# Modulation sections as one accumulating run of eight matmuls, in a diffusion backbone on one core

## The chip, the cores and the metric

The kernel runs on one NeuronCore of a Trainium2 chip. The metric is the device time of one execution in microseconds. Before the change it is 837.59 us, the median of three runs between 837.31 and 838.25.

## The reference

Two layers work on 512 latent tokens and 256 context tokens of width 1024. Each layer normalizes its input, scales and shifts it, mixes tokens, and adds a gated, normalized result:

```python
shift, scale, gate = adaln(c, ada_w[i], ada_b[i])        # silu(c) @ w + b, split in three
cshift, cscale, cgate = adaln(c_ctx, ada_w[i], ada_b[i])
h = rms_norm(x, pre_g[i]) * (1.0 + scale) + shift
y, yc = mixer_i(h, hc, ...)                               # 0: differential attention, 1: grouped-query attention
x = x + gate * rms_norm(y, post_g[i])
```

The change concerns `adaln`, the modulation: two vectors of 1024 (`c` and `c_ctx`) times a matrix of 1024 x 3072 per layer, in float32.

## The kernel before

**Tiling.** Activations lie with features on the 128 partitions, in eight blocks (`KT`). A weight block is loaded as float32 (`raw`, two buffers), split by a cast on ScalarE (`whi`, line 206) and a subtraction on GpSimd or VectorE (`wlo`, line 200), and used in three matmuls per block (lines 146 to 148, `mm3`). All weight loads are issued on SP's queue in a fixed order (`WStream`); three pairs of split buffers hold them, and a pair is refilled when its last matmul has released it.

**Stages.** First come the normalization and the modulation of layer 0's shift and scale (`ada_pe`, `cols4`, line 462). Then, up to about 470 us, layer 0's attention, where the change is. Then the output projection of layer 0, the whole of layer 1, and its output projection.

**Layer 0's attention.** Eight heads, one after the other. A unit is 128 queries against all keys: 12 score matmuls into a pair of double banks (line 868), two row maxima on VectorE (873), two exponentials on ScalarE (876), reciprocals, a scaling on GpSimd (214) and a combination on VectorE (884) that gives the probabilities `p`. Both double banks are used by each unit, so the next unit's scores need both exponentials done. Two units' probabilities are transposed on TensorE (line 933), evicted as a split pair `ah` (ScalarE, 936) and `al` (VectorE, 937), and multiplied with the values (line 153). At the end of a head a column sum of squares (lines 374 and 375, with ScalarE and GpSimd making its split pair in lines 372 and 373) normalizes the head's output. In between, as filler, TensorE projects the queries, keys, values and gates of later heads.

**What sets the order.** A planner (`flow`) keeps a clock of planned TensorE time and calls steps when they are due; each step has a cost, lags behind other steps and a time `at`. Fillers run when nothing is due. Single banks are handed out in rotation, the least recently used first (`trp` and `pj`, four banks). What the planner emits is then put into each engine's queue by a list scheduler that uses priorities and its own timeline. Each engine runs its queue in order.

**The modulation's later sections.** The six remaining sections of 512 columns (gates of layer 0, shift and scale of layer 1) are computed during heads 2 to 7. A section is two groups (`g`) of four matmuls, each group over 512 input features; `grp_load` loads 1 MB per group into `araw` (one buffer), on SP's queue. In `grp_mm` the four matmuls of a group go to the four column quarters of the array: matmul `j` multiplies the 32-column stationary `s32[:, 4*g+j]` with 512 columns and writes partitions 32j to 32j+31 of one bank. `after(prev)` keeps the four in order; other TensorE work may be placed between them. The first group's bank is copied to `arow` by ScalarE (line 727), the second group's bank is added to it by VectorE (line 730). Then the group's buffer is loaded again. `ada1_finish` (line 737) and `gate0_finish` (line 1002) sum the four quarters with one more matmul each and put the result into its place. `ACCN` says how many of these steps go to which head: three in each of heads 2 to 7 (two `grp_mm`, one finish), spaced evenly over the head.

Of the kernel before, what the change touches and what calls it, by code (L numbers as in the profile page):

```python
# [9 lines left out]
F32 = mybir.dt.float32  # L10
F32R = mybir.dt.float32r
AF = mybir.ActivationFunctionType
ALU = mybir.AluOpType
# [3 lines left out]
P = 128  # L17
# [12 lines left out]
HF0 = ((('qk', 1), ('qk', 2), ('z', 0)), (('qk', 3),), (('z', 1), ('v', 2), ('qk', 4), ('z', 2)), (('qk', 5), ('z', 3)), (('v', 4), ('qk', 6), ('z', 4)), (('qk', 7), ('z', 5)), (('v', 6), ('z', 6)), (('z', 7),))  # L30
FILL0 = tuple(f for hf in HF0 for f in hf)
ATT = 15.0
ACCN = (0, 0, 3, 3, 3, 3, 3, 3)
ACD = 5.0
FILL1 = (('z', 0), ('q', 2), ('q', 1), ('z', 2), ('z', 1), ('q', 3), ('z', 3), ('z', 4), ('z', 5), ('z', 7), ('z', 6))
HOT0 = (4200, 3100, 0, 4800)
# [48 lines left out]
def tile_backbone(  # L85
# [20 lines left out]
    nc = tc.nc  # L106
    uid = [0]

    def nm(s):
        uid[0] += 1  # L110
        return f"{s}_{uid[0]}"
# [178 lines left out]
    def after(prev):  # L290
        return nullcontext() if prev is None else tc.issue_after(prev.ins)
# [123 lines left out]
    def mod_cols(layer, half, which, psrc):  # L415
        for v in range(2):
            src = psrc(v)
            dst = mods[:, layer, v, which, half * 4:half * 4 + 4]
            b = abT[:, layer, which, half * 4:half * 4 + 4]
            if which == 0:  # L420
                nc.vector.tensor_tensor(dst, src, b, ALU.add)
            else:
                nc.vector.scalar_tensor_tensor(dst, src, 1.0, b, ALU.add, ALU.add)
                nc.vector.tensor_tensor(dst, dst, pre[:, layer, half * 4:half * 4 + 4], ALU.mult)
# [24 lines left out]
    s32 = cp.tile([P, KT, 32], F32, name="s32", bufs=1)  # L449
# [254 lines left out]

    with tc.tile_pool(name="t0", bufs=1) as t0:
        SECS = ((0, 4), (0, 5), (1, 0), (1, 2), (1, 1), (1, 3))
        groups = [(layer, sec, g) for layer, sec in SECS for g in range(2)]
        loaded, rows = {}, {}

        def grp_load(i):  # L710
            if i < len(groups):
                layer, sec, g = groups[i]
                t = loaded[i] = t0.tile([P, 4, 512], F32, tag="araw", name=nm("araw"), bufs=1)
                nc.sync.dma_start(
                    t, ada_w[layer, g * 512:(g + 1) * 512, sec * 512:(sec + 1) * 512].rearrange("(k p) n -> p k n", p=P))

        def grp_mm(i):
            layer, sec, g = groups[i]
            t = loaded.pop(i)
            o = trp()  # L720
            prev = None
            for j in range(4):
                with after(prev):
                    prev = nc.tensor.matmul(o[32 * j:32 * j + 32, :], s32[:, 4 * g + j, :], t[:, j, :], start=True, stop=True)
            if g == 0:
                r = rows[layer, sec] = t0.tile([P, 512], F32, tag="arow", name=nm("arow"), bufs=1)
                nc.scalar.copy(r, o)
            else:
                r = rows[layer, sec]
                nc.vector.tensor_tensor(r, o, r, ALU.add)  # L730
            grp_load(i + 1)

        def ada1_finish(layer, sec):
            r = rows.pop((layer, sec))
            o = trp()
            for b in range(4):
                nc.tensor.matmul(o[:, 2 * b:2 * b + 2], r[:, b * P:(b + 1) * P], sel32, start=b == 0, stop=b == 3)
            ov_ = o[:, :8].rearrange("p (k v) -> p v k", v=2)
            mod_cols(layer, sec % 2, sec // 2, lambda v: ov_[:, v, :])
# [30 lines left out]
        def qr_tile():  # L770
            return t0.tile([P, T], F32, tag="qr", name=nm("qr"), bufs=4)
# [223 lines left out]
        def gate0_finish(half):  # L995
            r = rows.pop((0, 4 + half))
            sl = slice(half * 512, half * 512 + 512)
            b = bcast(ada_b[0, 2 * D + half * 512:2 * D + half * 512 + 512])
            g = bcast(post_g[0, sl])
            for v in range(2):  # L1000
                o = trp()
                nc.tensor.matmul(o, selb[v], r, start=True, stop=True)
                nc.vector.tensor_tensor(gate0[v][:, sl], o, b, ALU.add)
                nc.vector.tensor_tensor(gate0[v][:, sl], gate0[v][:, sl], g, ALU.mult)
# [15 lines left out]
        for which, o in enumerate((oq, ok)):  # L1020
            r = qr_tile()
# [11 lines left out]
            add({"qk": qk_proj, "v": v_proj, "z": z_proj}[kind](i))  # L1033
        def acc_steps():
            res = []
            grp_load(0)
            for i, (layer, sec, g) in enumerate(groups):
                res.append(Step(lambda i=i: grp_mm(i), 1.5, hot=False))
                if g:
                    f = (lambda sec=sec: gate0_finish(sec - 4)) if layer == 0 else (lambda layer=layer, sec=sec: ada1_finish(layer, sec))  # L1040
                    res.append(Step(f, 2.0 if layer == 0 else 1.0, [(res[-1], ACD)], hot=False))
            return res

        A_ = acc_steps()
        S_, T_, M_, X_ = [], [], [], []
        at_ = clock[0] + FZ
# [38 lines left out]
        for h in range(KT):  # L1085
            per = ATT + DL0[h] + sum(7.7 if f[0] == 'z' else 15.4 for f in HF0[h] if f != ('qk', 1))
            span = per - GAP0
            lo, hi = sum(ACCN[:h]), sum(ACCN[:h + 1])
            for i in range(lo, min(hi, len(A_))):
# [35 lines left out]
            at_ += per  # L1125
        for st_ in A_[sum(ACCN):]:
            st_.at = at_
# [35 lines left out]
    for qi, (c, n) in enumerate(OUTC[:2]):  # L1163
# [4 lines left out]
        for m in order:  # L1168
            v = 0 if m < NQ else 1
            o = pj(n) if qi else o_pre[m]  # L1170
# [12 lines left out]
    c, n = OUTC[2]  # L1183
# [47 lines left out]
    for i, m in enumerate(order):  # L1231
        o = pj(n)
# [11 lines left out]
    with tc.tile_pool(name="t1", bufs=1, side="right") as t1p:  # L1244
# [61 lines left out]
        for what, m in KV:  # L1306
# [146 lines left out]
        def gate1_part(half, k2):  # L1453
            acc = gate1[:, half * 512:half * 512 + 512]
            gw = wp.tile([P, 1024], F32, tag="raw", name=nm("raw"), bufs=2)
            nc.sync.dma_start(
                gw.rearrange("p (k n) -> p k n", k=2),
                ada_w[1, k2 * 256:(k2 + 1) * 256, 2 * D + half * 512:2 * D + half * 512 + 512].rearrange("(k p) n -> p k n", p=P),
            )
            for k in range(2):  # L1460
                kt = k2 * 2 + k
                gs = gw[:, k * 512:(k + 1) * 512]
                if kt == 0:
                    VP[EGA].tensor_scalar(acc, gs, scol[:, 0, kt:kt + 1], None, ALU.mult)
                else:
                    VP[EGA].scalar_tensor_tensor(acc, gs, scol[:, 0, kt:kt + 1], acc, ALU.mult, ALU.add)

        def gate1_finish(half):
            acc = gate1[:, half * 512:half * 512 + 512]
            o = pj(512)  # L1470
            colsum(o, acc, [t1q.tile([P, 512], F32R, tag=t, name=nm("ac"), bufs=n) for t, n in (("za", 1), ("sz", 2))])
            b = wp.tile([P, 1024], F32, tag="raw", name=nm("raw"), bufs=2)
            sl = slice(half * 512, half * 512 + 512)
            nc.sync.dma_start(b[:, :512], ada_b[1, 2 * D + half * 512:2 * D + half * 512 + 512].partition_broadcast(P))
            nc.sync.dma_start(b[:, 512:], post_g[1, sl].partition_broadcast(P))
            nc.vector.tensor_tensor(acc, o, b[:, :512], ALU.add)
            close(o)
            nc.vector.tensor_tensor(acc, acc, b[:, 512:], ALU.mult)
# [33 lines left out]
        for h in range(KT):  # L1512
            p, j = h // 2, h % 2
# [17 lines left out]
        for i in range(10):  # L1531
            f = (lambda i=i: gate1_part(i // 5, i % 5)) if i % 5 < 4 else (lambda i=i: gate1_finish(i // 5))
# [10 lines left out]
        for qi, (c, n) in enumerate(OUTC1):  # L1543
# [4 lines left out]
            for m in range(NQ):  # L1548
                o = pj(n) if qi else o_pre[m]
# [12 lines left out]
                if qi == 2:  # L1562
                    r = rstd_sum(ss[m][:, 2:3], ss[m][:, 0:1])
# [95 lines left out]
```

## Time and profile before

| | |
|---|---|
| median of three runs | 837.59 us |
| the profiled execution, its own time | 836.02 us |
| its span, first to last instruction | 834.0 us |
| mean granted TensorE clock | 0.992 |
| TensorE busy | 797.1 us, 96% of the span |
| VectorE, ScalarE, GpSimd busy | 58%, 55%, 52% |
| line 724, the sections' matmuls | 48 matmuls, 96 records, from 163.7 to 421 us |
| line 730, VectorE's additions | 6 of about 0.69 us |
| line 714, the sections' loads | 12 of 1 MB, 5.5 us from issue to landing |

The span is shorter than the execution's own time by 2.0 us, which lie around it. In the profile a float32 matmul stands as two records, one for each pass, and each record's length is a modelled time from start to end; matmuls overlap, so distances between starts tell what one costs. "Busy" adds up stretches in which at least one instruction runs. In the rows of the timeline the first number is the start in us, the second the length in us; "x8" is the number of records merged in a row. In rows that group instructions by line, three numbers with slashes are the shortest, median and longest duration in ns. In the waits, the numbers are the total in us, how often, and the longest in us.

### The profile page before, as it was taken

How to read it: one execution, taken by the hardware profiler on the slowest of the kernel's cores; microseconds unless marked ns; L12 is line 12 of the kernel's file. 1: busy time of each engine (PE TensorE's matmuls, PEld its weight loads, DVE VectorE, ACT ScalarE, POOL GpSimd, SP SyncE). 2: the span in 40 equal slices, each digit the busy share in tenths (PEclk: the TensorE clock that was granted, in tenths of full speed). 3: DMA queues.
4: the chain of work that ended last, by engine and by line, in shares of the span. 5: the costliest groups of instructions: out<-in, count | busy, mean ns of one | idle time of the engine just before them, and what ended most of it. 6: DMA issues, size and time to landing. Idle time of an engine off the chain costs nothing. (4 is left out here: it accounts for less than half of the span.)

```text
span 834.0 us, 14405 instructions
## 1 busy us (share of the span) xinstructions
PE 797.1 (96%) x5482; PEld 705.2 (85%) x5482; DVE 484.2 (58%) x897; ACT 458.7 (55%) x1001; POOL 437.0 (52%) x538
## 2 busy tenths in 40 slices
PE   7999999999999999999999999989998989999997
PEld 5788887798878898778988898779998779889986
DVE  4434576764857425665377843674266677665634
ACT  5424357674574644764467643754364656666731
POOL 4444755865475743765633212585776836723201
PEclk9899999999999999999999999999999999999999
DMA  9934211222133321414310051031232240300112
GB/s 302 353 112 140 76 39 47 63 95 70 71 102 127 114 76 64 151 42 153 124 51 26 27 202 51 26 108 51 77 99 79 81 153 21 102 26 26 64 38 101
DMA packets 41540, 77.77 MB, mean 93 GB/s; under 512 B 3584, under 2 KB 18688, under 8 KB 41472
## 3 DMA queue, kind: packets, MB, share of 16 engines
q1 hardware_dynamic: 38048, 71.71, 26.0%
q10 hardware_dynamic: 3424, 5.15, 1.8%
q8 instruction: 43, 0.70, 0.3%
q14 instruction: 25, 0.20, 0.1%
HBM read 70.56 MB, written 2.10 MB: 87 GB/s over the span
## 5 line engine op out<-in xcount | busy, mean ns | idle before, releaser
L200 POOL TENSOR_TENSOR wlo<-raw,whi 128x256 fp32r<-128x256 f32 x200 | 150.6, 784 | 89.1 <-ACT whi L206 75.6
L146 PE MATMUL bk<-whi,h 128*128 128x256 f32 (+1 forms) x592 | 177.0, 302 | 6.2 <-DVE u L1191 1.8
L147 PE MATMUL bk<-wlo,h 128*128 128x256 f32 (+1 forms) x592 | 176.3, 299 | 0.2 <-DVE wlo L200 0.2
L148 PE MATMUL bk<-whi,h 128*128 128x256 f32 (+1 forms) x592 | 175.0, 298 | 0.9 <-DVE h L1229 0.8
L146 PE MATMUL bk<-h,whi 128*128 128x512 f32 (+2 forms) x416 | 147.7, 355 | 2.4 <-ACT sq L965 1.5
L148 PE MATMUL bk<-h,wlo 128*128 128x512 f32 (+2 forms) x416 | 144.9, 349 | 0.1
L147 PE MATMUL bk<-h,whi 128*128 128x512 f32 (+2 forms) x416 | 144.9, 349 | 0.0
L146 PEld LDWEIGHTS bk<-whi,h 128*128 128x128 f32 x592 | 112.6, 190 | 16.4 <-issue 4.2
L147 PEld LDWEIGHTS bk<-wlo,h 128*128 128x128 f32 x592 | 112.6, 190 | 4.3 <-issue 0.5
L148 PEld LDWEIGHTS bk<-whi,h 128*128 128x128 f32 x592 | 111.9, 190 | 5.1 <-DVE h L1229 1.5
L214 POOL TENSOR_SCALAR p<-p,sm 128x768 f32<-128x768 f32 (+1 forms) x80 | 68.2, 855 | 82.0 <-DVE sm L879 34.6
L146 PEld LDWEIGHTS bk<-h,whi 128*128 128x128 f32 x416 | 78.2, 188 | 15.3 <-issue 4.5
L206 ACT CAST whi<-raw 128x1024 fp32r<-128x1024 f32 x64 | 67.4, 1053 | 37.2 <-DMA raw<-in_b_w 15.1
L148 PEld LDWEIGHTS bk<-h,wlo 128*128 128x128 f32 x416 | 78.1, 188 | 8.7 <-issue 1.3
L147 PEld LDWEIGHTS bk<-h,whi 128*128 128x128 f32 x416 | 78.3, 188 | 7.0 <-issue 0.8
L876 ACT ACTIVATE p<-sc,sm 128x768 f32<-128x768 f32 (+1 forms) x68 | 59.7, 882 | 29.4 <-DVE sm L873 28.7
L873 DVE TENSOR_REDUCE sm<-sc 128x1 f32<-128x768 f32 (+1 forms) x68 | 60.5, 919 | 22.2 <-PE sc L868 22.2
L184 POOL TENSOR_TENSOR sz<-sz,za 128x384 f32<-128x384 f32 (+1 forms) x24 | 28.1, 1173 | 39.3 <-ACT za L183 39.3
L936 ACT CAST ah<-bk 128x512 fp32r<-128x512 f32 x56 | 31.8, 592 | 29.5 <-PE bk L933 23.6
L937 DVE TENSOR_TENSOR al<-bk,ah 128x512 fp32r<-128x512 f32 x56 | 37.6, 684 | 16.0 <-ACT ah L936 15.5
L868 PE MATMUL sc<-qk,qk 64*128 64x384 f32 (+1 forms) x396 | 46.1, 355 | 0.2 <-POOL qk L768 0.2
L1430 DVE TENSOR_TENSOR al<-bk,ah 128x512 fp32r<-128x512 f32 x48 | 32.3, 685 | 23.0 <-ACT ah L1429 23.0
(245 smaller groups left out, 1700.1 us busy)
## 6 DMA issues: line engine op xcount, KB each, us to landing
raw<-in_a_w SPq DMA_DIRECT2D x30, 512.0 KB, 3.6
araw<-in_ada_w SPq DMA_DIRECT2D x12, 1024.0 KB, 5.5
raw<-in_b_w SPq DMA_DIRECT2D x20, 512.0 KB, 3.5
ag<-in_ada_w SPq DMA_DIRECT2D x32, 256.0 KB, 6.7
raw<-in_w_out SPq DMA_DIRECT2D x16, 512.0 KB, 3.5
sw<-qr ACTq DMA_DIRECT2D x32, 128.0 KB, 2.1
raw<-in_ada_w SPq DMA_DIRECT2D x8, 512.0 KB, 3.6
xt<-in_x SPq DMA_DIRECT2D x4, 512.0 KB, 5.3
```

Of the source, the lines that this page charges most:

```text
L146: nc.tensor.matmul(o, ahi, bhi, start=start, stop=False)
L147: nc.tensor.matmul(o, ahi, blo, start=False, stop=False)
L148: nc.tensor.matmul(o, alo, bhi, start=False, stop=stop)
L200: eng.tensor_tensor(dst[:, i:i + n], a[:, i:i + n], b[:, i:i + n], op)
L206: nc.scalar.copy(hi, r)
L214: (nc.vector if eng == "v" else nc.gpsimd).tensor_scalar(dst, src, s_, 1.0, ALU.mult, ALU.mult)
L868: prev = nc.tensor.matmul(sc[m][:, j if nk == T else m, :w], a[r, tok], b[r, c], start=i == 0, stop=i == 2)
L873: nc.vector.tensor_reduce(mx, scv, AX.XY if nk == T else AX.X, ALU.max, negate=True)
L876: nc.scalar.activation(pv_, scv, AF.Exp, bias=mx, accum_out=l[:, m:m + 1])
L936: nc.scalar.copy(ah, tr)
L937: nc.vector.tensor_tensor(al, tr, f32(ah), ALU.subtract)
L1430: nc.vector.tensor_tensor(al, tr, f32(ah), ALU.subtract)
```

## The change

One step now computes a whole section: eight matmuls, two to each column quarter, of which the second accumulates onto the first in the same bank (`start` only for `g == 0`, `stop` only for `g == 1`). The section's two loads are issued one after the other into two `araw` buffers. One copy by ScalarE evicts the bank; the addition by VectorE is gone. The step costs 2.2 in the planner's clock where the two steps cost 1.5 each, and `ACCN` gives two steps per head instead of three.

```diff
-ACCN = (0, 0, 3, 3, 3, 3, 3, 3)
+ACCN = (0, 0, 2, 2, 2, 2, 2, 2)
...
-        def grp_load(i):
-            if i < len(groups):
-                layer, sec, g = groups[i]
-                t = loaded[i] = t0.tile([P, 4, 512], F32, tag="araw", name=nm("araw"), bufs=1)
-                nc.sync.dma_start(
-                    t, ada_w[layer, g * 512:(g + 1) * 512, sec * 512:(sec + 1) * 512].rearrange("(k p) n -> p k n", p=P))
-
-        def grp_mm(i):
-            layer, sec, g = groups[i]
-            t = loaded.pop(i)
+        def sec_load(i):
+            if i < len(SECS):
+                layer, sec = SECS[i]
+                loaded[i] = [t0.tile([P, 4, 512], F32, tag="araw", name=nm("araw"), bufs=2) for _ in range(2)]
+                for g, t in enumerate(loaded[i]):
+                    nc.sync.dma_start(
+                        t, ada_w[layer, g * 512:(g + 1) * 512, sec * 512:(sec + 1) * 512].rearrange("(k p) n -> p k n", p=P))
+
+        def sec_mm(i):
             o = trp()
             prev = None
-            for j in range(4):
-                with after(prev):
-                    prev = nc.tensor.matmul(o[32 * j:32 * j + 32, :], s32[:, 4 * g + j, :], t[:, j, :], start=True, stop=True)
-            if g == 0:
-                r = rows[layer, sec] = t0.tile([P, 512], F32, tag="arow", name=nm("arow"), bufs=1)
-                nc.scalar.copy(r, o)
-            else:
-                r = rows[layer, sec]
-                nc.vector.tensor_tensor(r, o, r, ALU.add)
-            grp_load(i + 1)
+            for g, t in enumerate(loaded.pop(i)):
+                for j in range(4):
+                    with after(prev):
+                        prev = nc.tensor.matmul(
+                            o[32 * j:32 * j + 32, :], s32[:, 4 * g + j, :], t[:, j, :], start=g == 0, stop=g == 1)
+            r = rows[SECS[i]] = t0.tile([P, 512], F32, tag="arow", name=nm("arow"), bufs=1)
+            nc.scalar.copy(r, o)
+            sec_load(i + 1)
...
-            for i, (layer, sec, g) in enumerate(groups):
-                res.append(Step(lambda i=i: grp_mm(i), 1.5, hot=False))
-                if g:
...
+            for i, (layer, sec) in enumerate(SECS):
+                res.append(Step(lambda i=i: sec_mm(i), 2.2, hot=False))
...
```

The finishing step follows each section's step as before.

More of the change, by code (lines that the diff above doesn't have):

```diff
@@ L706, in tile_backbone @@
         SECS = ((0, 4), (0, 5), (1, 0), (1, 2), (1, 1), (1, 3))
-        groups = [(layer, sec, g) for layer, sec in SECS for g in range(2)]
         loaded, rows = {}, {}
-        def grp_load(i):
-            if i < len(groups):
-                layer, sec, g = groups[i]
-                t = loaded[i] = t0.tile([P, 4, 512], F32, tag="araw", name=nm("araw"), bufs=1)
-                nc.sync.dma_start(
-                    t, ada_w[layer, g * 512:(g + 1) * 512, sec * 512:(sec + 1) * 512].rearrange("(k p) n -> p k n", p=P))
-        def grp_mm(i):
-            layer, sec, g = groups[i]
-            t = loaded.pop(i)
+        def sec_load(i):
[6 more added lines that the diff above has]
+        def sec_mm(i):
             o = trp()
             prev = None
-            for j in range(4):
-                with after(prev):
-                    prev = nc.tensor.matmul(o[32 * j:32 * j + 32, :], s32[:, 4 * g + j, :], t[:, j, :], start=True, stop=True)
-            if g == 0:
-                r = rows[layer, sec] = t0.tile([P, 512], F32, tag="arow", name=nm("arow"), bufs=1)
-                nc.scalar.copy(r, o)
-            else:
-                r = rows[layer, sec]
-                nc.vector.tensor_tensor(r, o, r, ALU.add)
-            grp_load(i + 1)
+            for g, t in enumerate(loaded.pop(i)):
[6 more added lines that the diff above has]
+            sec_load(i + 1)
         def ada1_finish(layer, sec):
@@ L1035, in acc_steps @@
             res = []
-            grp_load(0)
-            for i, (layer, sec, g) in enumerate(groups):
-                res.append(Step(lambda i=i: grp_mm(i), 1.5, hot=False))
-                if g:
-                    f = (lambda sec=sec: gate0_finish(sec - 4)) if layer == 0 else (lambda layer=layer, sec=sec: ada1_finish(layer, sec))
-                    res.append(Step(f, 2.0 if layer == 0 else 1.0, [(res[-1], ACD)], hot=False))
+            sec_load(0)
+            for i, (layer, sec) in enumerate(SECS):
+                res.append(Step(lambda i=i: sec_mm(i), 2.2, hot=False))
+                f = (lambda sec=sec: gate0_finish(sec - 4)) if layer == 0 else (lambda layer=layer, sec=sec: ada1_finish(layer, sec))
+                res.append(Step(f, 2.0 if layer == 0 else 1.0, [(res[-1], ACD)], hot=False))
             return res
```

## The prediction

> **What bounds the kernel now.** I read the page's busy shares first, then the busy times of the stretch that holds the change, then TensorE's waits in it.
>
> ```profile
> PE 797.1 (96%) x5482; PEld 705.2 (85%) x5482; DVE 484.2 (58%) x897; ACT 458.7 (55%) x1001; POOL 437.0 (52%) x538
> PEclk9899999999999999999999999999999999999999
> ```
>
> ```profile
> 110.00:430.00 320.00, 316.07 (x2228) 272.08 (x2227) 190.41 (x332) 187.12 (x393) 193.82 (x193) 1.00 0.27 88
> 430.00:470.00 40.00, 36.55 (x269) 33.88 (x267) 35.25 (x60) 30.26 (x64) 11.41 (x11) 1.00 0.08 27
> ```
>
> ```profile
> PE bk L933 <- DVE al L937: 1.9, 2, 1.6
> PE bk L375 <- POOL sqs L373: 1.6, 1, 1.6
> PE bk L146 <- ACT sq L965: 1.5, 1, 1.5
> PE bk L724 <- DVE al L937: 0.9, 1, 0.9
> PE bk L724 <- DVE gT L214: 0.6, 1, 0.6
> ...
> PE sc L868 <- POOL qk L768: 0.2, 1, 0.2
> ```
>
> The windows give length, then busy time of TensorE, its weight loads, VectorE, ScalarE and GpSimd. TensorE is the bound, and the clock granted to it is full (1.00 in both windows): in layer 0's attention it is idle for 320 - 316.07 = 3.9 us of 320, and in the last head (430 to 470 us) for 3.4 of 40. The waits (total, times, longest, from 67 to 470 us) explain most of it. No other engine passes 61% up to 430 us; in the last head VectorE reaches 35.25 of 40, so an eviction there waits its turn. So two things move the time: how long TensorE's own instructions take, and new or removed waits, which can save at most these 7.4 us.
>
> **The matmuls of the modulation.** They are 48 before and after, each a float32 matmul of 512 columns on one quarter of the array, recorded as two passes. Layer 0's first sections do the changed form already (L462): eight matmuls (x8 records are four matmuls, x16 eight) accumulating in one bank.
>
> ```profile
> 27.07 0.28 PE L148 MATMUL bk<-whi,h 128*128 128x256 f32 x1
> 27.28 1.06 PE L462 MATMUL bk<-ag,s 128*32 128x512 f32 x8
> 28.27 0.39 PE L146 MATMUL bk<-whi,h 128*128 128x256 f32 x1
> 28.61 0.28 PE L148 MATMUL bk<-whi,h 128*128 128x256 f32 x1
> ...
> 37.05 0.28 PE L147 MATMUL bk<-wlo,h 128*128 128x256 f32 x1
> 37.17 0.28 PE L148 MATMUL bk<-whi,h 128*128 128x256 f32 x1
> 37.37 1.92 PE L462 MATMUL bk<-ag,s 128*32 128x512 f32 x16
> 39.23 0.51 PE L146 MATMUL sc<-h,whi 128*128 128x256 f32 x2
> 39.57 0.28 PE L146 MATMUL bk<-whi,h 128*128 128x256 f32 x1
> ```
>
> ```profile
> 247.56 1.06 PE L724 MATMUL bk<-araw,s 128*32 128x512 f32 x6
> 248.55 0.66 PE L933 MATMUL bk<-ident,p 128*128 128x128 f32 x4
> 249.13 1.04 PE L724 MATMUL bk<-araw,s 128*32 128x512 f32 x2
> 250.11 0.50 PE L146 MATMUL bk<-h,whi 128*128 128x512 f32 x1
> ```
>
> Projection matmuls of 256 columns follow each other every 0.12 us (37.05, 37.17). From the L148 at 27.07 to the one at 28.61 are three such steps, 0.36 us; 1.54 passed, so a group of four costs 1.18. From 37.17 to 39.57 are again three steps; 2.40 passed, so a run of eight costs 2.04. The second four in a run thus cost 0.86, and getting in and out of the form 0.32. Whole runs would cost 6 x 2.04 = 12.2 us, against 12 x 1.18 = 14.2 for twelve whole groups.
>
> But neither program keeps them whole. The split group at 247.56 shows the price: its lone fourth matmul holds TensorE from 249.13 to 250.11, 0.98 us, as long as four (27.28 to 28.27). What counts is rounds of up to four quarters. The changed program's order on TensorE splits four of the six runs: 3+5, 6+2, 8, 4+4, 6+2, 8 matmuls, with scores, transposes or column sums between the parts. That is 10 entries and 3+3+2+2+3+2 = 15 rounds, against 13 entries and 13 rounds now (eleven groups of four, one of 3+1). Before: 13 x 1.18 = 15.3; after: 10 x 1.18 + 5 x 0.86 = 16.1. **+0.8 us**: the run costs more than the groups it replaces.
>
> Counting the changes of form alone, the sum would be 3 x 0.32 = 1.0 us less. The Trainium skill (TensorEngine Tiling (Array Packing), Key Properties) says that changing the tiling mode drains TensorE, and that tiles work independently; the 0.32 us agrees with the drain, and the lone matmul's 0.98 says that an unfilled round eats what the fewer drains save.
>
> **Banks, the copy and the add.** Each section takes one bank where it took two.
>
> ```profile
> L727 ACT COPY arow<-bk x6: 576/587/609, 166.4 to 411.9; 128x512 f32<-128x512 f32 x6
> L730 DVE TENSOR_TENSOR arow<-bk,arow x6: 676/688/692, 193.7 to 422.7; 128x512 f32<-128x512 f32 x6
> ```
>
> The six adds go: 6 x 0.69 = 4.1 us of VectorE, beside TensorE and worth nothing by themselves; the six copies stay. The two waits of L724 for a bank (0.9 and 0.6 above) should go: in the changed order at least 3 us of TensorE work lie between a bank's former use and a section's first matmul. Ends 0 and -1.5; I take **-1.5**.
>
> **Loads.** Twelve of 1 MB stay twelve, on SP's queue, but a section's two now stand together and wait for the former section's last matmuls. What is behind them are weight loads.
>
> ```profile
> araw<-in_ada_w SPq DMA_DIRECT2D x12, 1024.0 KB, 5.5
> raw<-in_a_w SPq DMA_DIRECT2D x30, 512.0 KB, 3.6
> L206 ACT CAST whi<-raw 128x1024 fp32r<-128x1024 f32 x64 | 67.4, 1053 | 37.2 <-DMA raw<-in_b_w 15.1 <-PE bk L147 10.2 <-PE bk L148 7.6
> 128.88 2.81 POOL L200 TENSOR_TENSOR wlo<-raw,whi 128x256 fp32r<-128x256 f32 x4 [1.21 <-ACT whi L206]
> ```
>
> ```profile
> SPq L714 <- PE bk L724: 73.2, 10, 22.0
> ```
>
> SP stands 73.2 us at these loads now, up to 22 at once, and no row of TensorE's waits in that stretch names a weight or araw. From the release, two loads, a weight load, cast and four subtractions take 2 x 5.5 + 3.6 + 1.05 + 2.8 (the four took 2.81 us at 128.88) = 18.5 us. In the new order at least 256 TensorE instructions, 0.12 us or more each, so some 31 us, stand between a section's last matmul and the first use of the weight behind the next pair. Price **0**; with the cover gone, one late load is 5.5 us. The second buffer itself gains nothing for the same reason: nothing waits for araw. The Trainium skill (Trainium Kernel Development and Optimization, Best Practices) says to double-buffer for performance; its gain here would be the wait for araw, and the waits above show none.
>
> **The order of everything else.** The planner has two steps per section in place of three, and the scheduler writes a new order for all engines from the first scores to the end of the last head: TensorE's first 3,131 of 5,343 instructions are affected; the rest stands as it was. Here the sign is decided. The chain that a new order can cut too short runs from a unit's scores to its free banks and its finished probabilities:
>
> ```profile
> 187.37 1.32 PE L868 MATMUL sc<-qk,qk 64*128 64x384 f32 x12
> 190.87 0.92 ACT L876 ACTIVATE p<-sc,sm 128x768 f32<-128x768 f32 x1
> 192.38 1.02 DVE L884 SCALAR_TENSOR_TENSOR p<-p,sm,p 128x768 f32<-128x768 f32 x1
> ...
> 442.39 1.33 PE L868 MATMUL sc<-qk,qk 64*128 64x384 f32 x12
> 447.21 0.90 ACT L876 ACTIVATE p<-sc,sm 128x768 f32<-128x768 f32 x1
> 449.34 1.75 DVE L884 SCALAR_TENSOR_TENSOR p<-p,sm,p 128x768 f32<-128x768 f32 x1 [0.75 <-POOL p L214]
> ```
>
> ```profile
> L936 ACT CAST ah<-bk x55: 567/589/623, 105.1 to 467.4; 128x512 fp32r<-128x512 f32 x55
> L937 DVE TENSOR_TENSOR al<-bk,ah x55: 674/683/693, 105.8 to 469.9; 128x512 fp32r<-128x512 f32 x55
> L373 POOL TENSOR_TENSOR sqs<-sq,sqs x14: 1001/1012/1609, 131.6 to 449.3; 128x384 fp32r<-128x384 f32 x14
> ```
>
> From the scores' end (188.69; 443.72) the second exponential frees the banks 3.1 and 4.4 us later, and probabilities are ready after 4.7 and 7.4.
>
> - Last head: between the second and the third unit's scores stand 3 transposes and 14 matmuls of 0.12 to 0.14 us, 2.1 us, where the old order had 4 transposes, 24 projection matmuls and 12 others. Short of the chain by 1.0 to 2.3. Just behind, a column sum's second half follows its first at once, which needs L373's 1.0 us (the wait of 1.6 above is such a place). Together 2.0 to 3.9, or 0 if another wait covers them: **+2.5**.
> - Second head: 4 transposes and 13 matmuls, 2.1 us, between its first two units. Today's shortest such place (about 2.6 us) waited 0.2 (the L868 row of the waits); 0.2 to 2.3: **+1.2**, the middle.
> - Probability matmuls: six follow their transposes by 1.1 to 2.4 us, where the old order's closest is 2.5; the eviction needs 0.59 + 0.68, more behind other work. 0 to 2.0: **+0.8**.
> - The transposes' 1.6 us wait at L937 in the last head loses its place: **-1.6**. The other two above may stay or go: 0 to -3.1.
>
> **Sum.** 0.8 - 1.5 + 2.5 + 1.2 + 0.8 - 1.6 = **+2.2 us**. The profiled execution took 836.0 us (span 834.0), 1.6 below the median of 837.59; on its own time that is 838.2, on the median 839.8. All low ends: 0.8 - 1.5 + 0 + 0.2 + 0 - 1.6 - 3.1 = -5.2; all high ends: 0.8 + 0 + 3.9 + 2.3 + 2.0 - 0 = +9.0; neither will come all at once.
>
> **Rivals.**
> - *Bank relief, faster.* With six takings of a bank fewer, the bank waits go (L724 1.5, L933 1.6, L965 1.5) and the new tight places cost nothing: 0.8 - 4.6 = -3.8, so 833.8. For it: places where a bank is taken again within 1.5 us fall from 11 to 5 in the new order. Against it: the chains above. It decides once the tight places cost under 2 us.
> - *No change.* The short chains come out shorter than the shortest I saw; 0.8 - 1.5 leaves -0.7: 836.9. For it: 2.1 us is within 1 us of the shortest chain.
> - *Late weight, slower.* The pair of loads ahead of a weight makes one late once, +5.5 on top of +2.2: 845.3. Against it: 31 us of cover.
>
> **How the numbers follow.** About 0.2% is what a measurement of this kernel can tell from no change, 1.7 us. Forecast (839.3 to 843.5) 0.43, late weight 0.08, bank relief 0.27, no change 0.22. Slower 0.51, same 0.22, faster 0.27. The range, 834.2 to 845.0, leaves out the ends of relief and of lateness.
>
> **What would show it.** Right: about 10 entries of the section matmuls in the timeline, with the partial ones of 1 us; no wait of them for a bank; one wait of 1 us or more at scores (L868's successor) in the last head, and more idle time there than 3.4 us. Wrong: TensorE idle under 5 us from 110 to 470, or a wait for a weight, or a changed clock.

## The result and the profile after

The changed kernel takes **845.72 us** (median of six runs, 843.94 to 847.30); the kernel before took 837.75 beside it (six runs, 837.31 to 838.41). The ratio is 1.0099, with a 95% interval from 1.0086 to 1.0112: 0.9 to 1.1% slower. Forecast were 839.8 us and at most 845.0. The sign was right, the size was not: 8.0 us in place of 2.2.

The profiled execution of the changed kernel took 843.94 us. From its page, the span and TensorE's busy time:

```profile
span 842.2 us, 14398 instructions
PE 800.8 (95%) x5482; PEld 707.7 (84%) x5482; DVE 482.3 (57%) x891; ACT 457.8 (54%) x1001; POOL 435.9 (52%) x538
```

The span grew by 8.2 us (834.0 before). TensorE is idle for 41.4 us of it (842.2 - 800.8) and was for 36.9: +4.5. Its busy time grew by 3.7, though it does the same 5,482 recorded matmuls. So there are two things to find, idle time and slower work. First from the start to TensorE's first instruction that differs in order, and from there to where the order is the same again, for the kernel before and then for the changed one (length, then busy times of TensorE, weight loads, VectorE, ScalarE, GpSimd, and the clock):

```profile
0.00:81.64 81.64, 74.65 (x497) 60.58 (x497) 33.95 (x73) 36.79 (x68) 36.21 (x58) 0.96 0.71 229
81.64:485.77 404.13, 394.71 (x2777) 342.54 (x2776) 251.11 (x429) 236.25 (x494) 230.02 (x229) 1.00 0.24 79
```

```profile
0.00:80.82 80.82, 74.09 (x498) 60.22 (x499) 30.85 (x72) 36.76 (x68) 35.88 (x58) 0.98 0.74 247
80.82:493.02 412.20, 398.79 (x2776) 345.30 (x2775) 251.53 (x425) 234.95 (x491) 230.11 (x229) 1.00 0.22 74
```

The stretch with the new order takes 8.1 us more, 4.0 of idle time and 4.1 of busy time. Ahead of it the changed kernel is 0.8 us faster, behind it 0.9 slower. By parts of layer 0's attention, again first before, then after:

```profile
110.00:200.00 90.00, 87.57 (x639) 76.34 (x638) 59.33 (x103) 56.85 (x122) 56.96 (x55) 1.00 0.18 59
200.00:250.00 50.00, 50.00 (x329) 41.22 (x327) 30.97 (x56) 33.02 (x71) 31.02 (x35) 1.00 0.24 80
350.00:430.00 80.00, 79.41 (x573) 68.71 (x566) 45.37 (x79) 43.83 (x92) 47.30 (x46) 1.00 0.33 106
```

```profile
110.00:200.00 90.00, 85.05 (x611) 72.92 (x611) 59.47 (x104) 56.22 (x121) 54.70 (x54) 1.00 0.18 61
200.00:250.00 50.00, 47.72 (x315) 39.90 (x315) 29.20 (x52) 26.58 (x55) 27.03 (x30) 0.97 0.19 60
350.00:430.00 80.00, 77.79 (x551) 66.50 (x550) 44.05 (x69) 44.59 (x90) 50.73 (x49) 1.00 0.28 95
438.00:478.00 40.00, 38.05 (x278) 34.15 (x277) 35.45 (x63) 31.66 (x65) 12.29 (x11) 1.00 0.08 28
```

Idle time rose from 2.4 to 4.9 us in the second and third heads (110 to 200), from nothing to 2.3 where the first gate is finished (200 to 250), and from 0.6 to 2.2 between 350 and 430. In the last head, whose work now stands some 8 us later, it fell from 3.4 (430 to 470) to 2.0. TensorE's waits between 67 and 480 us (total, times, longest):

```profile
PE bk L929 <- DVE al L933: 2.1, 3, 1.4
PE bk L929 <- DVE p L880: 1.5, 2, 1.2
PE bk L153 <- DVE al L933: 1.5, 2, 1.1
PE bk L146 <- DVE al L933: 1.5, 1, 1.5
PE bk L146 <- DVE gT L214: 1.4, 2, 0.9
PE bk L929 <- DVE gate L999: 1.3, 1, 1.3
PE sc L864 <- POOL qk L764: 1.2, 1, 1.2
PE bk L153 <- DVE sm L875: 0.9, 1, 0.9
PE bk L153 <- ACT ah L932: 0.8, 1, 0.8
```

It is another set of waits (line 929 here is 933 before, 933 is 937, 864 is 868). The two of the sections' matmuls for a bank are gone, and no row names a weight or araw. Two places that the prediction named are among them, one between two units' scores in the second head and one in the last:

```profile
129.77 0.51 PE L153 MATMUL bk<-ah,vhi 128*128 128x256 f32 x2 [1.10 <-DVE al L933]
448.91 0.51 PE L153 MATMUL bk<-ah,vhi 128*128 128x256 f32 x2 [0.81 <-ACT ah L932]
451.10 0.50 PE L153 MATMUL bk<-al,vhi 128*128 128x256 f32 x2 [0.43 <-DVE al L933]
451.86 1.32 PE L864 MATMUL sc<-qk,qk 64*128 64x384 f32 x12 [0.26 <-ACT p L872]
```

The largest single place is one that the prediction does not have: the finish of the first gate. TensorE, then VectorE, in the timeline (start, length, what; in brackets the idle time before it and what ended it):

```profile
215.98 1.12 PE L998 MATMUL bk<-arow,selb 128*128 128x512 f32 x2
216.94 0.60 PE L929 MATMUL bk<-ident,p 128*128 128x128 f32 x4
218.88 0.66 PE L929 MATMUL bk<-ident,p 128*128 128x128 f32 x4 [1.34 <-DVE gate L999]
220.44 0.48 PE L153 MATMUL bk<-ah,vhi 128*128 128x256 f32 x2 [0.90 <-DVE sm L875]
```

```profile
216.23 0.95 DVE L869 TENSOR_REDUCE sm<-sc 128x1 f32<-128x768 f32 x1
217.10 1.13 DVE L757 TENSOR_TENSOR sw<-sw,rope 128x512 f32<-128x512 f32 x1
218.15 0.68 DVE L999 TENSOR_TENSOR gate<-bk,raw 128x512 f32<-128x512 f32 x1
218.75 0.94 DVE L869 TENSOR_REDUCE sm<-sc 128x1 f32<-128x768 f32 x1
219.62 0.68 DVE L999 TENSOR_TENSOR gate<-bk,raw 128x512 f32<-128x512 f32 x1
```

The gate's sum over the four quarters takes one matmul and one bank for each of the two vectors (`c` and `c_ctx`). In the old order they are TensorE's instructions 1300 and 1378; now they are 1300 and 1301. Two of four banks are taken at once, and VectorE, which must free them, has a maximum and a rotary product queued ahead: the first bank is free at 218.8, the second at 220.3. (The profile puts the second wait down to a reciprocal that VectorE does just behind that, at 220.2; the end of the second gate row is 0.1 us earlier.) Windows of these five microseconds, and of the 3.4 us behind them:

```profile
215.00:220.00 5.00, 3.15 (x12) 1.33 (x11) 4.77 (x7) 1.90 (x5) 2.54 (x2) 1.00 0.08 28
221.40:224.80 3.40, 3.40 (x18) 3.18 (x19) 2.61 (x6) 0.38 (x1) 0.32 (x1) 0.50 0.75 270
```

VectorE is busy 4.77 us of 5, TensorE 3.15. Then the granted clock falls to 0.50 for 3.4 us, in which half of the time is lost: another 1.7 us. The clock stood at 1.00 in this stage before.

Over the whole execution, though, the clock comes out even: the kernel before has 6.8 us of half clock at 18 us, where the changed one has 3.4 at 30, and both have 3.4 once more behind 630. Both profiled executions have a mean clock of 0.992, so the 1.7 us count inside the stretch and not for the whole execution.

The 4.1 us of busy time in the stretch are 1.7 of half clock, 0.7 of the sections' matmuls (below), 1.0 of the transposes (from each record's start to the next, idle time taken off, their 224 records take 24.1 us in place of 23.1) and 0.7 of the gate's own matmuls (8 records, 3.0 us in place of 2.3). Why these last two got slower, no run shows.

### The profile page after: what moved, and what is told of

It reads as the page before. It is cut to its first block, busy times and chain, and to the rows that moved or that the text cites. A ratio compares the mean times of both kernels' runs of the same rounds, so it can differ in the third digit from the quotient of the medians.

```text
span 842.2 us, 14398 instructions
## 1 busy us (share of the span) xinstructions
PE 800.8 (95%) x5482; PEld 707.7 (84%) x5482; DVE 482.3 (57%) x891; ACT 457.8 (54%) x1001; POOL 435.9 (52%) x538
## 5 line engine op out<-in xcount | busy, mean ns | idle before, releaser
L200 POOL TENSOR_TENSOR wlo<-raw,whi 128x256 fp32r<-128x256 f32 x200 | 152.3, 793 | 65.9 <-ACT whi L206 56.2
L880 DVE SCALAR_TENSOR_TENSOR p<-p,sm,p 128x768 f32<-128x768 f32 (+1 forms) x34 | 40.2, 1181 | 15.8 <-POOL p L214 13.5
```

The costliest lines, as they stand in the source:

```text
L200: eng.tensor_tensor(dst[:, i:i + n], a[:, i:i + n], b[:, i:i + n], op)
L880: nc.vector.scalar_tensor_tensor(ps_[0], pt, r, ps_[0], ALU.mult, ALU.add)
```

## The experiments

Theory **order**: the section matmuls, banks and loads are worth a microsecond or two; the 8 us come from where everything else now stands, and from the half clock behind the new waits. Rivals: **form** (the run of eight, or the bank it holds, costs by itself), **loads** (the second buffer and its transfers), and the **gate's place** alone. No run here leaves out any computation.

### One bank for a section, nothing else

The kernel before, but the second group accumulates in the first one's bank; the addition goes. One load buffer, two steps as before.

```diff
-            o = trp()
+            if g == 0:
+                accb[0] = pj(512)
+            o = accb[0]
...
-... start=True, stop=True)
-            if g == 0:
+... start=g == 0, stop=g == 1)
+            if g == 1:
...
-                nc.vector.tensor_tensor(r, o, r, ALU.add)
+                close(o)
```

> The kernel before with one part of the change alone: the second group of four matmuls accumulates in the first one's bank, one copy by ScalarE, no addition by VectorE. Steps, planner costs and the single load buffer stay as before. Theory 'order' (the pieces of the change cost next to nothing, the new order of the whole attention stage costs the time): TensorE's order here differs from the one before only after instruction 986 and the sections keep 13 rounds; so within 3 us of the kernel before, 836 to 841 us, and what it loses shows as TensorE waits at new places. Theory 'accumulation' (accumulating in one bank itself is slow, or the bank held longer starves the other users): most of the 8 us is here, 843 us or more, with waits for banks all over the stage.

850.53 us, ratio 1.0149 (1.0120 to 1.0177): dearer than the whole change, and not the 836 to 841 that theory order gave; by its time alone it is on the side of the rival named there. Waits from 340 to 480 us:

```profile
PE bk L153 <- DVE al L938: 3.3, 2, 1.9
PE sc L869 <- ACT p L877: 3.1, 1, 3.1
PE bk L727 <- DMA araw<-in_ada_w: 2.6, 1, 2.6
PE bk L934 <- DVE gT L214: 1.7, 1, 1.7
```

Up to TensorE's instruction 2100 this run stands 0.7 us behind the kernel before, with three sections done in that form; all of its loss comes behind that, in places that have to do with no section, and at one load: with one buffer the second group's megabyte starts only when the first group's matmuls are done, and the order has them 7.7 us apart. So the waits don't stand all over the stage, as that rival had it, and holding the bank cost next to nothing through three sections. Whether the bank that is held makes the last heads come out tight, no run shows.

### Two load buffers, nothing else

```diff
-                t = loaded[i] = t0.tile([P, 4, 512], F32, tag="araw", name=nm("araw"), bufs=1)
+                t = loaded[i] = t0.tile([P, 4, 512], F32, tag="araw", name=nm("araw"), bufs=2)
...
-            grp_load(i + 1)
+            grp_load(i + 2)
...
             grp_load(0)
+            grp_load(1)
```

> The kernel before with two load buffers alone: each group's load is issued two groups ahead; matmuls, copies and additions are those of before. TensorE's order differs only between instructions 425 and 1321. Theory 'order': the loads cost nothing; what is lost is what the order up to 1321 costs, between 0 and 3 us: 837 to 841 us. Theory 'loads' (the second megabyte at the start of the stage or the weight loads behind the pair are late): 841 us or more, with TensorE or its weight loads waiting for wlo or whi.

839.93 us, ratio 1.0026 (1.0015 to 1.0038). No matmul waits for araw here or before, so nothing is gained. The early second load moves the scheduler's own timeline: the order differs from TensorE's instruction 425 to 1321, and the second head has three waits of the changed kernel and one much like its fourth (1.51, 1.09, 0.58 and 1.18 us between 119 and 164 us). So that part of the change can come from the load's place in the order alone; no wait here names the transfer.

### Whole runs of eight

The changed kernel, its eight matmuls at a priority that lets nothing in between.

```diff
+            with tc.high_priority(offset=9000):
               for g, t in enumerate(loaded.pop(i)):
```

> The changed kernel with the eight matmuls of a section at high priority, so that all six runs stay whole: 12 rounds and 6 entries in place of 15 and 10. By the rounds term the sections' matmuls cost 6 x 2.04 = 12.2 us instead of 16.1, so 3.9 us less, if that were all: 841.8 us. Theory 'order': the gate finish stays as it is in the changed kernel (both its matmuls next to each other at instruction 1300), so its wait of some 4 us stays; the rest is a new order, so 838 to 845 us, and the sections' own time falls by 2 us or more in the timeline.

848.91 us, ratio 1.0130 (1.0115 to 1.0145), above the 838 to 845 that was expected. The form does get cheaper: six runs of 1.85 us from the first start to the next instruction's, 11.1 us for all, where the kernel before has 12.9. But the order behind it has a wait of 3.4 us for scores in the last head, and four stretches of 3.41 us at half clock.

### The gate's finish in two steps

The changed kernel with the two gate matmuls planned as steps of their own (heads 2 and 3 then have three steps each).

```diff
-                f = (lambda sec=sec: gate0_finish(sec - 4)) if layer == 0 else ...
+                if layer == 0:
+                    for v in range(2):
+                        res.append(Step(lambda sec=sec, v=v: gate0_finish(sec - 4, v), 1.0, [(res[-1], ACD)], hot=False))
```

> The changed kernel with the gate's finish as two planner steps, one for each of its two matmuls, so that they no longer take two banks one right after the other (instructions 1154 and 1301 for the first section). Theory 'gate finish' (about half of the loss is the place at 217 us where TensorE stands behind the evictions of the gate's two banks and its clock falls): the jump of 4 us there goes, 840 to 842 us, and the granted clock there stays full. Rival: the wait only moves to another place of the new order, 844 us or more.

843.68 us, ratio 1.0081 (1.0060 to 1.0103), 2.0 under the changed kernel, and between the two forecasts (840 to 842, or 844 and more). The jump at the gate is gone (against the kernel before, 0.2 us between instructions 1260 and 1320 where the change lost 4.0). But the new order has lost 5 us by instruction 1140, and has a wait of 2.1 us at 368. The gate is a true part of the loss; of the 4.0 us taken out there, the new order lost half again elsewhere.

### The kernel before with another order

Here no instruction is added, removed or changed. First one cost in the planner, then one due time:

```diff
-                res.append(Step(lambda i=i: grp_mm(i), 1.5, hot=False))
+                res.append(Step(lambda i=i: grp_mm(i), 1.1, hot=False))
```

> The kernel before with one number of the planner changed (1.1 in place of 1.5 for a group's four matmuls); not one instruction is added, removed or changed, only the order on the engines differs, on TensorE from instruction 1159 to 4236. Theory 'order' (the section matmuls, banks and loads are worth under 1 us each; what the change costs is the waits of the new order and the half-clock stretches behind them): a planner-only perturbation of the kernel before costs some us too, 838 to 846, with new waits of over 1 us between 150 and 470 us that the kernel before has not. Rival 'form' (the run of eight, or the bank it holds, costs the 8 us): within 0.2% of the kernel before, 836 to 839.

```diff
-                A_[i].at = at_ + per * (i - lo + 0.5) / (hi - lo)
+                A_[i].at = at_ + per * (i - lo + 0.4) / (hi - lo)
```

> The kernel before with the section steps due a tenth of their spacing earlier (0.4 in place of 0.5); no instruction differs but in order, on TensorE from 979 to 3128. Theory 'order': 838 to 846, with waits of over 1 us in new places; the two conditional runs of it, this one and the one with cost 1.1, need not agree. Rival 'form': 836 to 839.

The first took **844.27 us, ratio 1.0090** (1.0064 to 1.0116), the second **845.32, ratio 1.0097** (1.0078 to 1.0116). Either loses about as much as the change does, with the old form, the old loads and the old banks. So a new order by itself can cost 8 us, and both runs are where theory order had them and rival form had not. The longest wait of the first, and of the second:

```profile
PE sc L868 <- ACT p L876: 3.4, 1, 3.4
```

```profile
PE bk L724 <- DMA araw<-in_ada_w: 2.3, 1, 2.3
```

The first is the chain from scores to free double banks, which the prediction named, in the last head (461.6 us). The second is a late load in the one-buffer form: it lands 8.4 us after its issue, with a weight load issued 0.4 us ahead of it, and the two groups stand 9.6 us apart.

### The changed kernel with other orders

One number each, the same instructions. The planner's cost of a section:

```diff
-                res.append(Step(lambda i=i: sec_mm(i), 2.2, hot=False))
+                res.append(Step(lambda i=i: sec_mm(i), 3.0, hot=False))
```

> The changed kernel with the planner told 3.0 in place of 2.2 for a run of eight; same instructions, another order. Theory 'order': it leaves the changed kernel's 845.7 by more than 2 us, either way (839 to 850). Rival 'form': within 1.5 us of the changed kernel. The gate's two matmuls stand 15 instructions apart here, so less than half of that place's wait of 2.2 us should be left.

and the steps' due time:

```diff
-                A_[i].at = at_ + per * (i - lo + 0.5) / (hi - lo)
+                A_[i].at = at_ + per * (i - lo + 0.67) / (hi - lo)
```

> The changed kernel with its section steps due later (0.67 of their spacing in place of 0.5), which sets the first gate's two matmuls 78 instructions apart as in the kernel before, and leaves the second head as in the changed kernel; 7 entries of the column-quarter form and 13 rounds in place of 10 and 15. Theory 'order': the gate's waits (1.3 and 0.9 us) and the half-clock stretch behind them go, 4 to 5.5 us; the matmuls gain 3 x 0.32 + 2 x 0.86 = 2.7 us by the prediction's prices; the second head's waits stay: 838 to 842 unless the new order has a new wait. Rival 'form': 843 to 846 less those 2.7.

846.86 us (ratio 1.0114, 1.0098 to 1.0129) and 844.33 (1.0080, 1.0063 to 1.0097). Both are misses. The first moved by only 1.1 us, within the 1.5 that rival form gave; its gate still waits 1.2 us, about half of the changed kernel's 2.2, and the last head's scores wait 3.0 us. The second did not come down to 842, and is above what the rival gave (843 to 846 less 2.7). The second is told apart by its trace. Instruction for instruction it is 0.5 us behind its start at TensorE's 2700th, so up to 425 us the changed form has lost nothing. Then it loses some 6 us up to the end of the last head:

```profile
PE sc L864 <- ACT p L872: 3.0, 1, 3.0
PE bk L146 <- DVE gT L214: 1.4, 1, 1.4
PE bk L929 <- DVE gT L214: 1.3, 1, 1.3
```

```profile
465.90:472.70 6.80, 5.45 (x27) 5.05 (x24) 6.77 (x12) 4.10 (x10) 5.02 (x3) 0.50 0.00 0
```

Waits of 5.7 us, and behind the longest a stretch of 6.8 us at half clock. The scores' wait is for the exponentials of the unit before, here ahead of the head's last, shorter unit; five of the runs in this document have it there, with 3.0 to 3.4 us, and the kernel before has none.

### The second load held back

To keep the second head's order, the first section's second load is made to depend on the second head: a one-column copy of a softmax sum into its buffer stands ahead of the transfer, which overwrites it.

```diff
-ACCN = (0, 0, 2, 2, 2, 2, 2, 2)
+ACCN = (0, 1, 2, 2, 2, 2, 2, 2)
...
+            if len(gs) == 1 and g == 1:
+                nc.vector.tensor_copy(t[:, 0, 0:1], lastl[0])
...
-            sec_load(0)
+            sec_load(0, (0,))
+            res.append(Step(lambda: sec_load(0, (1,)), 0.0, hot=False))
```

> The changed kernel, only that the second load of the first section is held back by a real dependency into the second head (a one-column copy of a softmax sum into its buffer goes ahead of it). TensorE's order is then the one of the kernel before up to instruction 950, and near the changed kernel's behind that, the two gate matmuls next to each other again (1300, 1301). Theory 'order': the second head's waits of the changed kernel (1.5, 1.1, 0.6 and 1.2 us between 115 and 165 us) go, the gate's waits stay: 2 to 3 us under the changed kernel, 842 to 844. Rival 'loads' (the second load costs by the transfer itself): the time hardly moves, since the same bytes go over the same queue: 845 to 847.

846.52 us, ratio 1.0105 (1.0088 to 1.0122): a miss, and in the range of rival loads, though no wait of TensorE there names a load. TensorE's order is the old one up to instruction 950, and the second head's waits are the old ones too. But 1.4, 0.9 and 1.2 us of waits for a bank or for scores come at 159 to 169 us in their place, and the gate is as bad as it was (1.5 and 0.9, half clock at 224).

With the due time at 0.67 on top:

> The same with the section steps due later (0.67): the gate's two matmuls 91 instructions apart, 9 entries of the column-quarter form and 15 rounds. Theory 'order': second head and gate both as in the kernel before, and in the last head a scores wait of 1 to 1.5 us in place of the 3.0 of the run with 0.67 alone: 837 to 841. Rival 'form': it stays at 843 or more.

845.77 us, ratio 1.0102 (1.0087 to 1.0117): a miss as well, in the range of rival form. The gate's waits are gone, the last head's scores wait 2.6 us and a transpose's bank 2.2. Then one number of this kernel changed:

```diff
-                res.append(Step(lambda i=i: sec_mm(i), 2.2, hot=False))
+                res.append(Step(lambda i=i: sec_mm(i), 2.0, hot=False))
```

> As the run before it with one number changed (the planner is told 2.0 in place of 2.2 for a run of eight). In its order no two units' scores stand closer on TensorE than in the kernel before, the gate's matmuls stand 91 apart, five of the six runs of eight are whole (7 entries, 13 rounds). Theory 'order': the waits over 1 us of the changed kernel are gone, and what is left is the form's own worth, by the prediction's prices 13 x 1.18 - (7 x 1.18 + 6 x 0.86) = 1.9 us of matmuls and 1.5 us of bank waits: 833 to 838. Rival 'form' (the run of eight costs by itself): 841 or more.

**838.54 us, ratio 1.0011** (0.9998 to 1.0024, ten runs): level with the kernel before, 7.2 us under the run with 2.2, and half a microsecond above the range forecast. The form, the held bank and the second buffer are all in it, so none of them costs 8 us by itself. Its page, and its waits from 110 to 480 us:

```profile
PE 796.0 (95%) x5482; PEld 706.3 (85%) x5482; DVE 481.1 (58%) x892; ACT 456.5 (55%) x1001; POOL 436.7 (52%) x538
```

```profile
PE bk L374 <- DVE gT L214: 1.9, 1, 1.9
PE bk L375 <- POOL sqs L373: 1.6, 1, 1.6
PE bk L146 <- ACT sq L967: 1.5, 1, 1.5
PE bk L146 <- DVE al L939: 1.4, 2, 1.1
PE bk L738 <- ACT sz L839: 1.2, 1, 1.2
```

TensorE is busy 1.1 us less than before (796.0 against 797.1) and idle 2.9 us more (835.8 - 796.0 = 39.8): a gain in busy time is there, less than the 1.9 that the form is worth by the prediction's prices, and waits that the kernel before hasn't (1.9, 1.4 and 1.2) eat it. Last, the order with all six runs whole:

```diff
-                res.append(Step(lambda i=i: sec_mm(i), 2.2, hot=False))
+                res.append(Step(lambda i=i: sec_mm(i), 1.6, hot=False))
...
-                A_[i].at = at_ + per * (i - lo + 0.67) / (hi - lo)
+                A_[i].at = at_ + per * (i - lo + (0.67 if h < 3 else 0.5)) / (hi - lo)
```

> As the run with 0.67 in the third head alone, 0.5 in the others and 1.6 told for a run of eight: all six runs whole (6 entries, 12 rounds), gate 91 apart, no scores closer than in the kernel before. Theory 'order': 833 to 838, by the prediction's prices 0.9 us under a kernel with 7 entries and 13 rounds and otherwise equal waits. Rival 'form': 841 or more.

843.42 us, ratio 1.0072 (1.0048 to 1.0096): a miss, in the range of rival form, though its six runs do take 11.1 us. Its order has a wait of 2.1 us for scores at 270 and 1.5 for a bank at 323, which a count of distances on TensorE had not shown.

| kernel | median us | span | TensorE idle in it | half-clock stretches, 60 to 510 us |
|---|---|---|---|---|
| before | 837.8 | 834.0 | 36.9 | 0 |
| changed | 845.7 | 842.2 | 41.4 | 1 |
| before, cost 1.1 | 844.3 | 841.0 | 40.9 | 2 |
| before, due 0.4 | 845.3 | 845.4 | 39.8 | 2 |
| changed, due 0.67 | 844.3 | 844.5 | 44.7 | 3 |
| changed, late load, due 0.67 | 845.8 | 842.4 | 42.1 | 1 |
| the same, cost 2.0 | 838.5 | 835.8 | 39.8 | 0 |

Span, idle time and stretches of 3.41 us are those of one profiled execution each; the median is over all runs.

What the runs show is this much: an order alone can cost what the change costs, and the form in a better order costs nothing. Most forecasts for a single order were missed, and all but one of the misses came out slower than forecast. The level order is one of nine tried with the new form; the other eight took 843.4 to 848.9 us. Of all the kernels here the one before is the fastest, so it is no surprise that another order loses. Whether the new form makes tight orders likelier than the old one does, four altered runs of the old kernel (839.9 to 850.5) are too few to tell.

## Why the prediction was right and wrong

**The matmuls of the modulation: right.** 0.8 us were forecast. Rows of the changed kernel, a split run's first part and a whole run, with what follows each:

```profile
177.69 1.06 PE L723 MATMUL bk<-araw,s 128*32 128x512 f32 x6
178.68 0.44 PE L146 MATMUL bk<-h,whi 128*128 128x384 f32 x1
...
302.13 1.92 PE L723 MATMUL bk<-araw,s 128*32 128x512 f32 x16
303.98 0.39 PE L147 MATMUL bk<-wlo,h 128*128 128x256 f32 x1
```

Three matmuls hold TensorE for 0.99 us, eight for 1.85. The ten parts sum to 14.2 us from start to next start, the thirteen before to 12.9; with the prediction's 0.18 around each (1.18 less 1.00), which was not measured again, it is 14.17 + 1.80 against 12.92 + 2.34, +0.7. Whole runs would have been worth 11.1 + 1.1 against 15.3, -3.1, as its 12.2 had it.

**Banks, the copy and the add: right.** Both waits of the sections' matmuls are gone, and the missing additions bought nothing.

**Loads: right for the time, wrong in a side remark.** No weight came late. But "the second buffer itself gains nothing" holds for the order of the kernel before only: in two other orders one buffer cost 2.6 and 2.3 us. And with two buffers alone the early load gave the second head a new order and new waits, which the step did not consider.

**The order of everything else: this step failed**, and not at the places that it named. It gave +2.9 us of waits (2.5 + 1.2 + 0.8 - 1.6), and with the banks' -1.5 that is 1.4 us of added idle time. The stretch has 4.0 of it, and 3.4 of half clock and slower rows on top.

- The named places came, a little smaller than priced. Between the first two units of the second head stands one wait of 1.1 us (1.2 forecast); between the second and third unit of the last head stand three, 1.5 us together (2.5 forecast), of which the scores' own is only 0.3. All probability matmuls that wait, without the gate's, are in these two places, so the 0.8 for them didn't come on top. The transposes' 1.6 went as forecast.
- It put the rest of the new order at nothing, and that is where the loss is. Of 13.1 us of waits over 0.15 us in the stretch, 10.5 are at places without a price: 2.2 at the gate's finish, 1.5 at 121.6 us, 1.4 at 368.9, 1.2 each at 105.8 and 162.6, and smaller ones. Nearly the whole old set, 9.1 us, went as well, where the prediction counted 3.1 of it as gone. The step looked at chains of scores, transposes and sums. A pair of matmuls that takes two of four banks while VectorE is full is of the same kind and was not looked for.
- It gave the clock no price and named a changed clock only as what would make it wrong. Half clock behind the gate cost 1.7 us in the profiled execution. In the medians the clock counts too: the six runs of the changed kernel have clocks of 0.992 to 0.988, which is 9.1 us of lost clock on average (the span times what is missing to full clock). The kernel before lost 7.0 to 7.6 in its runs beside the experiments, so some 2 of the 8 us are clock, by this estimate.

So for the stretch the sum should have been 0.7 for the matmuls, 4.0 for idle time with the banks' 1.5 already in it, 1.7 for the clock and 1.7 for slower transposes and gate matmuls: 8.1 us. The sign came out right in part by luck: with the named places alone, at what they measured, the sum is 0.7 - 1.5 + 2.6 - 1.6 = +0.2 us, which is no change.

Of the marks it set: ten entries and no bank wait of the sections came; the wait of 1 us at scores and more idle time in the last head did not; a changed clock did. The rival "bank relief" (0.27) was right about the banks and fails on the condition it named itself, that the new tight places cost under 2 us: the two named ones alone took 2.6.

**What stays open.** Whether some order of the changed form beats the kernel before: the best one found is level, with 2 us of gain eaten by waits. And why the transposes and the gate's matmuls take 1.7 us longer.

## What to carry to other kernels

When a scheduler writes the order, a change is measured together with a new order: change one number of the old kernel's planner first, and if that alone costs as much as the change, the result says little about the change. Judge the change by its own rows (here -3.1 to +0.7 us of matmuls, 1.5 of bank waits), and look for an order afterwards. A tight place is wherever TensorE takes more than one scarce bank within the time that a full VectorE needs to give one back, not only on the chains that waited before.

## What the runs showed of the hardware

The granted clock of TensorE falls to 0.50 for 3.41 us, or twice that, behind waits far shorter than that. After 1.34 and 0.90 us of waiting within 3 us it did so in the changed kernel. In the run with two load buffers alone, a transpose waits 1.56 us at 432.8, and the clock behind it is halved:

```profile
434.60:438.00 3.40, 3.40 (x18) 3.18 (x18) 2.80 (x8) 1.00 (x3) 0.91 (x1) 0.50 0.00 0
```

In the kernel before, the order there is the same, the wait is 1.57 us at 431.3, and the clock stays whole:

```profile
433.00:436.40 3.40, 3.40 (x30) 3.01 (x31) 3.10 (x9) 1.18 (x3) 0.91 (x1) 1.00 0.00 0
```

Within each of the 14 traces the half-clock stretches start on one grid of 3.41 us, and what they follow is TensorE's idle time within one cell of that grid: 1.8 us in the cell from 218.0 to 221.4 of the changed kernel. In these traces, between 60 and 800 us, half clock followed every cell with 1.9 us or more of idle time. No cell at full clock with less than 1.49 was followed by it, and between these some were and some weren't. The two waits above, 1.56 and 1.57 us, lie whole within one cell each, in the part where both happen. So a wait of that length costs itself, and sometimes 1.7 us more. Much of the spread between runs of one kernel looks like lost clock: the five runs of the order with six whole runs have spans from 837.6 us at a clock of 0.994 to 843.7 at 0.986. That is 5.0 and 11.8 us of lost clock, 6.8 apart, where the spans are 6.1 apart. The Trainium skill (TensorE: Matmul & The Clock Gate, What's actually happening) states that the clock is set by activity in windows of 3413 ns that run freely. The length of the stretches and their common grid agree with that. Its rule to have no idle gaps over some 3.4 us (HAM oscillation — how this bites in real kernels) is too lax here: 1.6 us in one piece, or 2.2 in two, were enough.
